# Six row buffers from the start of the expert gathers, weights in smaller pieces, and a new pacing table

## The chip, the cores and the metric

The kernel runs on one core of a Trainium2 chip. Its engines are TensorE (PE, with the weight loads as PEld), VectorE (DVE), ScalarE (ACT) and GpSimd (POOL); SyncE's queue (SP) issues most transfers. The metric is the device time of one execution in microseconds, and the kernel before is given by the median of three runs.

## The reference

One decoder block on 1024 tokens of width 1024, float32:

```
h = rms_norm(x);  proj = h @ w_in                    # 9232 columns
o_sb  = stick_breaking_attention(q, k, v)            # 8 heads of 128
o_gdn = gated_delta_rule(silu(conv(...)))            # 8 heads of 128, gates b and a
x = x + (sigmoid(g1) * (o_sb @ w1) + sigmoid(g2) * (o_gdn @ w2)) @ w_out
h = rms_norm(x)
# PEER: per token and head the best 16 of 128 x 128 experts (product keys)
expert, gate = route(h @ w_q, keys1, keys2)          # 8 heads x 16 = 128 experts a token
act = gelu(sum(h * u_tab[expert]))                   # 16384 rows of 1024 in each table
x = x + sum(gate * act * v_tab[expert])
```

## The kernel before, in words

The tokens are done in two halves of 512. A half goes through the stick-breaking heads (`sb_pair`), the delta-rule heads (`gdn_head`), the gate logits, the merge of both branches with their weights, the output projection, the norm ahead of the experts, and the routing (`route`, `route_block`). Matmuls take float32 operands split into a high and a low part, three products each (`mm3`); ACT makes the high part and DVE the low part (`split`, lines 63 and 64).

A weight slab of 1024 x 256 is loaded by `load_w` in two transfers of 512 KB into `w_raw` (two buffers of 4 KB a partition), split into `w_hi` and `w_lo` (two buffers each). There are 56 slabs in each half.

The expert part is done in two ways. Four of the eight token blocks (2, 3, 6, 7) are *dense*: `gate_table` writes a table of gates for all 16384 experts, and `dense` runs through all 128 groups of 128 experts: 24 matmuls for the scores of one group, 24 for its values. One group needs on DVE the low parts of the U and V slabs, the product with the gates (L915), the low part of the result (L906) and on average one addition to `d_acc` (L974). The other four blocks (0, 1, 4, 5) are *gathered* by `gather_rows`: for each of 128 expert columns POOL fetches 128 rows of the U table (512 KB, an indirect DMA, L1016) and DVE multiplies and sums them (L1019); then the same with the V table (L1021). That makes 4 x 256 = 1024 row fetches. Rows of block 0 exist when the first half is routed, so all rows run beside the second half and the dense part. Each row fetch lands in one of the buffers of `self.row_bufs` in turn: four of 4 KB a partition, and two more (`gp2`) while the dense loop runs.

What sets the order: the program is put into one order per engine by a scheduler that goes by priorities and its own costs. The rows get the lowest priority (`self.later(1000000)`), and a pacing table says how many of them become due at each step of the other work. `gather(phase)` adds `PACE[phase]` to `self.due`, and for each whole row puts one into the program, to stand on DVE behind the last DVE instruction issued so far (`self.behind`). The second half and the dense part call it 64 times in the stick-breaking heads, 80 in the delta rule, 16 each in logits, merge, output projection and routing, 64 in the gate tables and 128 in the dense loop. Rows left over at the end follow last. Each engine executes its order as written: an instruction that waits holds up all behind it on that engine, and so does a transfer in SP's queue that waits for its buffer.

In the second half's stick-breaking heads the keys and values of the first half come back from memory into `ko` and `vo` (256 KB each, two buffers). `gdn_head` keeps its tiles in the pool `gc`, two buffers a name, but one for `g_at` and `g_vn`. The residual `x2` has three of its four blocks in the pool `xp`, loaded during the merge, and the fourth in `fn`, loaded in front of the output projection. The raw V slabs of the dense part lie in the pool `up`, the split ones in `vp`, which opens after the routing buffers are given back (`gctx.close()`).

Of the kernel before, what the change touches and what calls it, by code (L numbers as in the profile page):

```python
# [7 lines left out]
F32 = mybir.dt.float32  # L8
# [10 lines left out]
P = 128  # L19
D = 1024  # L20
S = 1024
H = 8
TH = 512
NTB = TH // P
GT = 32
GQ = 4
KD = D // P
CB = 256
EPS = 1e-6

PACE = dict(sb=2.2, gdn=1.5, logits=2.5, merge=2.5, out=0.5, route=0, table=0.1, dense=5.25)
NEG = -1e30
C_Q, C_K, C_V = 0, 1024, 2048
C_GQ, C_GK, C_GV, C_GZ = 3072, 4096, 5120, 6144
# [4 lines left out]
class Block:  # L39
# [48 lines left out]
    def load_w(self, src, c0):  # L88


        hi = self.wp.tile([P, KD, CB], F32R, name="w_hi")
        lo = self.wp.tile([P, KD, CB], F32R, name="w_lo")
        for k0 in range(0, KD, 4):
            raw = self.wraw.tile([P, 4, CB], F32, name="w_raw")
            self.nc.sync.dma_start(raw, src[c0 // CB][:, k0:k0 + 4])
            for k in range(k0, k0 + 4, 2):
                self.split(hi[:, k:k + 2], lo[:, k:k + 2], raw[:, k - k0:k - k0 + 2])
        return hi, lo

    def load_ba(self):  # L100

        hi, lo = [self.wp.tile([P, KD, CB], F32R, name=f"w_{a}")[:, :, 0:16] for a in ("hi", "lo")]
        raw = self.wraw.tile([P, 4, CB], F32, name="w_raw").rearrange("p a b -> p (a b)")[:, 0:16 * KD]
        raw = raw.rearrange("p (k n) -> p k n", k=KD)
        self.nc.sync.dma_start(raw, self.i["w_ba"])
        self.split(hi, lo, raw)
        return hi, lo
# [233 lines left out]
    def sb_pair(self, half, pair, kqv):  # L341
        nc = self.nc
        k, q, v = kqv
        for h in range(2):
            kts = [k[:, h, j * P:(j + 1) * P] for j in range(NTB)]
            vs = [v[:, j, h * P:(h + 1) * P] for j in range(NTB)]
            if half:
                ko = self.ch.tile([P, TH], F32, name="ko", bufs=2)
                nc.sync.dma_start(ko, self.k_old[pair][:, h])
                vo = self.ch.tile([P, NTB, P], F32, name="vo", bufs=2)  # L350
                nc.sync.dma_start(vo, self.v_old[pair][:, :, h * P:(h + 1) * P])
                kts = [ko[:, j * P:(j + 1) * P] for j in range(NTB)] + kts
                vs = [vo[:, j] for j in range(NTB)] + vs
            self.sb_attend(half, pair * 2 + h, q[:, h], kts, vs)
# [96 lines left out]
    def gdn_head(self, half, head, G, r):  # L451
        nc, pool, mm = self.nc, self.ch, self.nc.tensor.matmul
        qT, kT, vT, sz = r["q"], r["k"], r["v"], r["z"]
        f = lambda a: a.rearrange("p a b -> p (a b)")
        tb_sl = lambda a, c: a[:, c * P:(c + 1) * P]
        col = lambda nm, c: G[nm][:, c, head:head + 1]
        W = lambda nm, **kw: pool.tile([P, NTB, P], F32, name=nm, **kw)
# [43 lines left out]
        M = W("g_M")  # L501
# [4 lines left out]
        TT, TN = W("g_TT"), W("g_TN")  # L506
# [30 lines left out]
        pq = pg()  # L537
        for c in range(NTB):
            mm(pq[:, c], tb_sl(kT, c), tb_sl(qT, c), start=True, stop=True)
        at = W("g_at", bufs=1)  # L540
        nc.vector.tensor_tensor(at, pq, dec, op=OP.mult)

        vn = W("g_vn", bufs=1)
        p2 = pg()
        for c in range(NTB):
            nc.tensor.transpose(p2[:, c], tb_sl(vT, c), self.ident)
# [307 lines left out]
    def dense(self, hx, blks, G, routes, gctx):  # L854
# [3 lines left out]
        W = nb * P  # L858
# [4 lines left out]
        with ExitStack() as ctx:  # L863
            pool = lambda *a, **k: ctx.enter_context(self.tc.tile_pool(*a, reuse_waits="tile", **k))
            up = pool(name="up", bufs=2)
# [63 lines left out]
            def values(vp):  # L929

                k = len(Vs)
                e1, dh = k // (2 * G) * G + k % G, k // G % 2
                raw = up.tile([P, 2, 512], F32, name="v_raw")
                nc.sync.dma_start(raw, V[e1 // 2, dh])
                v2 = [vp.tile([P, 2, 512], F32R, name=f"d_v{a}", bufs=VB // 2) for a in range(2)]
                self.split(v2[0], v2[1], raw)
                Vs.extend([[a[:, q] for a in v2] for q in range(2)])
# [19 lines left out]
            gctx.close()  # L957
            vp = pool(name="vp", bufs=2)
            acc = vp.tile([P, nb, D], F32, name="d_acc", bufs=1)
            gp2 = pool(name="gp2", bufs=1)  # L960
            self.row_bufs += [(gp2, f"gb_row{4 + k}") for k in range(2)]
            for k in range(0, VB, 2):
                values(vp)
            for k in range(LEAD):
                weigh(vp)
            for k in range(2 * NE1):
# [11 lines left out]
                if k % 2 == 1:  # L978
# [6 lines left out]
                    self.gather("dense")  # L985
                    if len(Vs) < 2 * NE1:
                        values(vp)
            del self.row_bufs[4:]
            for n, blk in enumerate(blks):
                nc.sync.dma_start(self.out[0, blk * P:(blk + 1) * P, :], acc[:, n])  # L990

# [1 line left out]
    def gather_rows(self, blks):  # L993

        nc = self.nc
        n = H * 16
        self.row_bufs = [(self.gp, f"gb_row{k}") for k in range(4)]
        turn = 0
        for blk in blks:
            h2 = self.gp.tile([P, D], F32, name="gb_h2", bufs=1)  # L1000
            nc.sync.dma_start(h2, self.h2_d[blk])
            act = self.gp.tile([P, n], F32, name="gb_act")
            ix = self.expert[blk]
            acc = None
            for p in range(2 * n):
                if p == n:
                    self.acts(nc.scalar.activation(act, act, AF.Gelu))
                    self.back_to_exp()
                    nc.vector.tensor_tensor(act, act, self.gate[blk], op=OP.mult)
                    acc = self.gp.tile([P, D], F32, name="gb_h2", bufs=1)  # L1010
                    nc.sync.dma_start(acc, self.x2_d[blk])
                pool, name = self.row_bufs[turn % len(self.row_bufs)]
                turn += 1
                r = pool.tile([P, D], F32, name=name, bufs=1)
                q = p % n
                nc.gpsimd.indirect_dma_start(out=r, out_offset=None, in_=self.i["peer_u" if p < n else "peer_v"][0],  # L1016
                                             in_offset=bass.IndirectOffsetOnAxis(ap=ix[:, q:q + 1], axis=0))
                if p < n:
                    i = nc.vector.scalar_tensor_tensor(r, r, 1.0, h2, op0=OP.mult, op1=OP.mult, accum_out=act[:, q:q + 1])  # L1019
                else:  # L1020
                    i = nc.vector.scalar_tensor_tensor(acc, r, act[:, q:q + 1], acc, op0=OP.mult, op1=OP.add)  # L1021
                if self.anchor is not None:
                    self.behind(i, self.anchor)
                if p == 2 * n - 1:
                    nc.sync.dma_start(self.out[0, blk * P:(blk + 1) * P, :], acc)
                yield
# [34 lines left out]
    def half(self, half, hx, new_h, st, x2_in):  # L1061

        nc, tc = self.nc, self.tc
        tp = lambda name, **k: tc.tile_pool(name=name, bufs=1, reuse_waits="tile", **k)
        if x2_in is None:
            self.mixers(half, hx)
        xctx = ExitStack()
        xp = xctx.enter_context(tp("xp", side="right"))
        x2 = [xp.tile([P, D], F32, name=f"x2{tb}") for tb in range(3)]
        if x2_in is None:  # L1070
            with tp("mo") as mo:
                mg = new_h()
                self.merge(half, mg, x2, mo)
        hb = st.enter_context(tp("hb"))
        with tp("rt") as rt:
            with tp("fn") as fn:
                x2 += [fn.tile([P, D], F32, name=f"x2{tb}") for tb in range(3, NTB)]
                if x2_in is None:
                    self.load_x(half, x2, range(3, NTB))
                    self.out_proj(half, mg, x2)  # L1080
                else:
                    for tb in range(NTB):
                        nc.sync.dma_start(x2[tb], x2_in[0, half * TH + tb * P:half * TH + (tb + 1) * P])
                self.keysT = rt.tile([P, H, 2, P], F32, name="keysT")
                nc.sync.dma_start(self.keysT, self.i["keys_t"])
                hf = [hb.tile([P, KD, TH], F32R, name=f"hf{a}") for a in range(2)]
                self.ffn_norm(half, x2, hf, fn)
            xctx.close()
            with tp("rq") as rq:
                routes = self.route(half, hf, rq)  # L1090
                if half == 0 and x2_in is None:
                    with tp("nin") as nin:
                        hx = new_h()
                        self.norm_in(1, hx, nin)
        return hf, hx, routes


def block_kernel(tc, ins, out, x2_in=None, dense_blks=(2, 3, 6, 7), G=8):
    b = Block(tc, ins, out)
    b.dense_blks = list(dense_blks)  # L1100
    nc = tc.nc
    with ExitStack() as ctx:
        pool = lambda *a, **k: ctx.enter_context(tc.tile_pool(*a, **k))
# [19 lines left out]
        with ExitStack() as rctx:  # L1123
            right = lambda name, bufs: rctx.enter_context(tc.tile_pool(name=name, bufs=bufs, side="right"))
            cm = right("cm", 1)
            hp = right("hp", 1)
            b.wp = right("wp", 2)
            b.wraw = right("wraw", 2)
            new_h = lambda: [hp.tile([P, KD, TH], F32R, name=f"h{a}") for a in range(2)]
            with tc.tile_pool(name="ctmp", bufs=1) as tp:  # L1130
                b.consts_first(cp, tp)
# [47 lines left out]
```

## Time and profile before

| | us |
|---|---|
| median of 3 runs (3879.04 to 3883.69) | 3883.02 |
| profiled execution | 3877.26 |
| its span, first to last instruction | 3875.4 |
| PE busy | 3596.4 |
| DVE busy | 3077.5 |
| ACT busy | 1740.7 |
| POOL busy | 1356.6 |

The second half starts its heads near 1015 us, the gate tables run from 2142 to 2373 us and the dense loop from there to the end. In the rows, an engine's busy time is followed by the number of its instructions in brackets; PEclk is the granted TensorE clock as a share of full speed; a group of instructions shows its busy time, the mean of one in ns, and the idle time of its engine just before it with what ended that.

### The profile page before, as it was taken

How to read it: one execution, taken by the hardware profiler on the slowest of the kernel's cores; microseconds unless marked ns; L12 is line 12 of the kernel's file. 1: busy time of each engine (PE TensorE's matmuls, PEld its weight loads, DVE VectorE, ACT ScalarE, POOL GpSimd, SP SyncE). 2: the span in 40 equal slices, each digit the busy share in tenths (PEclk: the TensorE clock that was granted, in tenths of full speed). 3: DMA queues.
4: the chain of work that ended last, by engine and by line, in shares of the span. 5: the costliest groups of instructions: out<-in, count | busy, mean ns of one | idle time of the engine just before them, and what ended most of it. 6: DMA issues, size and time to landing. Idle time of an engine off the chain costs nothing.

```text
span 3875.4 us, 53560 instructions
## 1 busy us (share of the span) xinstructions
PE 3596.4 (93%) x18936; PEld 2983.8 (77%) x18936; DVE 3077.5 (79%) x6196; ACT 1740.7 (45%) x3846; POOL 1356.6 (35%) x1034
## 2 busy tenths in 40 slices
PE   8999999999999999998878877999999999999996
PEld 7878888788777688886667666787778787788785
DVE  5345554349988878888879998899898899899898
ACT  6755554333777655553322786222222322222221
POOL 0000000000044332223442003666666665676665
PEclk9999999999999999999989999999999999999998
DMA  4221113553377756558985568999999999999998
GB/s 121 88 82 50 55 50 115 174 186 93 96 256 265 246 191 192 191 182 290 325 307 170 158 185 289 353 361 358 334 365 358 345 371 365 348 364 374 353 359 312
DMA packets 344205, 937.49 MB, mean 242 GB/s; under 512 B 41984, under 2 KB 121088, under 8 KB 339712
## 3 DMA queue, kind: packets, MB, share of 16 engines
q0 software_dynamic: 147456, 536.94, 38.8%
q1 hardware_dynamic: 196480, 397.13, 30.1%
q8 instruction: 149, 2.44, 0.3%
q14 instruction: 120, 0.98, 0.1%
HBM read 864.22 MB, written 69.21 MB: 241 GB/s over the span
## 4 chain that ended last, share of the span: by engine, by line
PE 42%; issue 20%; POOL 12%; DVE 11%; DMA 10%; ACT 4%; SPq 0%; POOLq 0%; DVEq 0%; ACTq 0%
POOL gb_row L1016 12%; PE mm L72 6%; PE mm L74 6%; PE mm L73 6%; DMA gb_row<-peer_v,expert 5%; PE pc L848 3%; DMA gb_row<-peer_u,expert 3%; PE mm L885 2%; PE pz L532 2%; PE pz L526 2%; DVE gb_row L1019 2%; DVE w_lo L64 2%; PE mm L887 1%; PE pc L317 1%; PE pz L295 1%
## 5 line engine op out<-in xcount | busy, mean ns | idle before, releaser
L1016 POOL DMA_INDIRECT gb_row<-peer_u,expert x512 | 693.6, 1355 | 1848.2 <-DVE expert L793 1012.8
L1016 POOL DMA_INDIRECT gb_row<-peer_v,expert x512 | 661.9, 1293 | 656.4 <-DVE gb_h L1021 408.8
L1019 DVE SCALAR_TENSOR_TENSOR gb_row<-gb_row,gb_h 128x1024 f32<-128x1024 f32 x512 | 614.0, 1219 | 133.2 <-DMA gb_row<-peer_u,expert 109.7
L1021 DVE SCALAR_TENSOR_TENSOR gb_h<-gb_row,gb_act,gb_h 128x1024 f32<-128x1024 f32 x512 | 657.7, 1285 | 73.7 <-DMA gb_row<-peer_v,expert 50.4
L885 PE MATMUL mm<-hf,ut 128*128 128x512 f32 x2048 | 491.2, 391 | 6.9 <-DMA hf<-hd 6.9
L919 ACT CAST d_a<-u_act 128x512 fp32r<-128x512 f32 x128 | 79.2, 621 | 926.5 <-DVE u_act L915 917.7
L885 PEld LDWEIGHTS mm<-hf,ut 128*128 128x128 f32 x2048 | 386.1, 189 | 87.7 <-issue 7.6
L64 DVE TENSOR_TENSOR w_lo<-w_raw,w_hi 128x512 fp32r<-128x512 f32 (+1 forms) x450 | 297.6, 682 | 163.9 <-ACT w_hi L63 125.9
L63 ACT CAST w_hi<-w_raw 128x512 fp32r<-128x512 f32 (+1 forms) x450 | 262.1, 620 | 286.2 <-PE mm L73 122.6
L72 PE MATMUL mm<-h,w_hi 128*128 128x512 f32 (+1 forms) x784 | 322.9, 412 | 3.0 <-ACT pj L598 3.0
L74 PE MATMUL mm<-h,w_lo 128*128 128x512 f32 (+1 forms) x784 | 320.6, 409 | 0.0
L73 PE MATMUL mm<-h,w_hi 128*128 128x512 f32 (+1 forms) x784 | 319.7, 408 | 0.0
L72 PE MATMUL pz<-d_v,d_a 128*128 128x512 f32 x680 | 272.8, 401 | 41.2 <-DVE d_acc L974 30.1
L72 PE MATMUL mm<-w_hi,h 128*128 128x256 f32 x1024 | 299.8, 293 | 8.5 <-DVE x L647 5.7
L74 PE MATMUL mm<-w_hi,h 128*128 128x256 f32 x1024 | 294.0, 288 | 4.0 <-DVE h L64 4.0
L73 PE MATMUL mm<-w_lo,h 128*128 128x256 f32 x1024 | 295.1, 288 | 1.0 <-DVE w_lo L64 0.9
L74 PE MATMUL pz<-d_v,d_a 128*128 128x512 f32 x680 | 270.4, 398 | 0.0
L73 PE MATMUL pz<-d_v,d_a 128*128 128x512 f32 x680 | 270.4, 398 | 0.0
L887 PE MATMUL mm<-hf,ut 128*128 128x512 f32 x1024 | 257.0, 391 | 2.5 <-DVE ut L64 2.5
L887 PEld LDWEIGHTS mm<-hf,ut 128*128 128x128 f32 x1024 | 192.8, 188 | 42.8 <-DVE ut L64 3.3
L72 PEld LDWEIGHTS mm<-w_hi,h 128*128 128x128 f32 x1024 | 199.5, 195 | 16.3 <-DVE x L647 6.4
L73 PEld LDWEIGHTS mm<-w_lo,h 128*128 128x128 f32 x1024 | 199.7, 195 | 6.7 <-issue 3.8
(327 smaller groups left out, 7947.9 us busy)
## 6 DMA issues: line engine op xcount, KB each, us to landing
w_raw<-w_in SPq DMA_DIRECT2D x144, 512.0 KB
u_raw<-u_t SPq DMA_DIRECT2D x128, 512.0 KB
v_raw<-v_t SPq DMA_DIRECT2D x128, 512.0 KB
g_d<-gt_stg SPq DMA_DIRECT2D x16, 2048.0 KB
d_g<-g_d SPq DMA_DIRECT2D x31, 1024.0 KB
w_raw<-peer_w_q SPq DMA_DIRECT2D x32, 512.0 KB
gl<-pj SPq DMA_DIRECT2D x32, 256.0 KB
th<-gl SPq DMA_DIRECT2D x32, 256.0 KB
```

The costliest lines, as they stand in the source:

```text
L63: nc.scalar.copy(hi, src)
L64: nc.vector.tensor_tensor(lo, src, hi.bitcast(F32), op=OP.subtract)
L72: mm(out, l[0], r[0], start=first, stop=False)
L73: mm(out, l[0], r[1], start=False, stop=False)
L74: mm(out, l[1], r[0], start=False, stop=last)
L848: self.last_gate = mm(pg[:, u - u0], o2[:, u], o1[:, u], start=True, stop=True)
L885: mm(ps, ut[0][:, k], hx[a][:, k, x0:], start=k + a == 0, stop=False)
L887: mm(ps, ut[1][:, k], hx[0][:, k, x0:], start=False, stop=k == KD - 1)
L919: nc.scalar.copy(hi, act)
L1016: nc.gpsimd.indirect_dma_start(out=r, out_offset=None, in_=self.i["peer_u" if p < n else "peer_v"][0], in_offset=bass.IndirectOffsetOnAxis ...
L1019: i = nc.vector.scalar_tensor_tensor(r, r, 1.0, h2, op0=OP.mult, op1=OP.mult, accum_out=act[:, q:q + 1])
L1021: i = nc.vector.scalar_tensor_tensor(acc, r, act[:, q:q + 1], acc, op0=OP.mult, op1=OP.add)
```

## The change

- `row_bufs` has six buffers from the start; `gp2` is gone. All six stay in use to the end.
- `w_raw` has three buffers of 2 KB a partition for two of 4 KB; a slab comes in four transfers of 256 KB.
- `ko` and `vo` have one buffer each. In `gdn_head`, `at` is written into `M` and `vn` into `TN`, whose last readers stand ahead of it.
- `xp` holds two blocks of `x2` for three; blocks 2 and 3 lie in `fn`.
- The raw V slabs lie in `vp`.
- The pacing table is new; with its numbers of calls, 404.8 rows are due ahead of the dense loop for 355.2.

```diff
-PACE = dict(sb=2.2, gdn=1.5, logits=2.5, merge=2.5, out=0.5, route=0, table=0.1, dense=5.25)
+PACE = dict(sb=2.4, gdn=2.0, logits=2, merge=2, out=0.5, route=0, table=0.3, dense=4.85)
...
-        for k0 in range(0, KD, 4):
-            raw = self.wraw.tile([P, 4, CB], F32, name="w_raw")
-            self.nc.sync.dma_start(raw, src[c0 // CB][:, k0:k0 + 4])
-            for k in range(k0, k0 + 4, 2):
-                self.split(hi[:, k:k + 2], lo[:, k:k + 2], raw[:, k - k0:k - k0 + 2])
+        for k in range(0, KD, 2):
+            raw = self.wraw.tile([P, 2, CB], F32, name="w_raw")
+            self.nc.sync.dma_start(raw, src[c0 // CB][:, k:k + 2])
+            self.split(hi[:, k:k + 2], lo[:, k:k + 2], raw)
...
-                ko = self.ch.tile([P, TH], F32, name="ko", bufs=2)
+                ko = self.ch.tile([P, TH], F32, name="ko", bufs=1)
-                vo = self.ch.tile([P, NTB, P], F32, name="vo", bufs=2)
+                vo = self.ch.tile([P, NTB, P], F32, name="vo", bufs=1)
...
-        at = W("g_at", bufs=1)
+        at = M
-        vn = W("g_vn", bufs=1)
+        vn = TN
...
-                raw = up.tile([P, 2, 512], F32, name="v_raw")
+                raw = vp.tile([P, 2, 512], F32, name="v_raw")
...
-            gp2 = pool(name="gp2", bufs=1)
-            self.row_bufs += [(gp2, f"gb_row{4 + k}") for k in range(2)]
-            del self.row_bufs[4:]
-        self.row_bufs = [(self.gp, f"gb_row{k}") for k in range(4)]
+        self.row_bufs = [(self.gp, f"gb_row{k}") for k in range(6)]
...
-        x2 = [xp.tile([P, D], F32, name=f"x2{tb}") for tb in range(3)]
+        x2 = [xp.tile([P, D], F32, name=f"x2{tb}") for tb in range(2)]
-                    self.load_x(half, x2, range(3, NTB))
+                    self.load_x(half, x2, range(2, NTB))
...
-            b.wraw = right("wraw", 2)
+            b.wraw = right("wraw", 3)
```

The first place is DVE in front of the second half's merge. `o` are the low parts of the attention output that the merge multiplies, `gb_row` the fetched rows, `part` the first product of the merge. Before, the last `o` stands 25 rows ahead of this piece:

```order
L1021 SCALAR_TENSOR_TENSOR gb_h_13437<-gb_row_16645,gb_act,gb_h_13437 128x1024
L783 TENSOR_TENSOR r_scr<-r_tab,r_i 128x1024
L1021 SCALAR_TENSOR_TENSOR gb_h_13437<-gb_row_16648,gb_act,gb_h_13437 128x1024
L785 TENSOR_REDUCE r_fa<-r_scr 128x64
L624 TENSOR_TENSOR part<-mm,th 128x512
```

The same place on DVE of the kernel after the change:

```order
L1017 SCALAR_TENSOR_TENSOR gb_h_13596<-gb_row_16613,gb_act,gb_h_13596 128x1024
L64 TENSOR_TENSOR o_18521<-o_raw,o_18520 128x512
L1017 SCALAR_TENSOR_TENSOR gb_h_13596<-gb_row_16632,gb_act,gb_h_13596 128x1024
L64 TENSOR_TENSOR o_18521<-o_raw,o_18520 128x512 x2
L1017 SCALAR_TENSOR_TENSOR gb_h_13596<-gb_row_16635,gb_act,gb_h_13596 128x1024
L64 TENSOR_TENSOR o_18521<-o_raw,o_18520 128x512
L1017 SCALAR_TENSOR_TENSOR gb_h_13596<-gb_row_16654,gb_act,gb_h_13596 128x1024
L1017 SCALAR_TENSOR_TENSOR gb_h_13596<-gb_row_16657,gb_act,gb_h_13596 128x1024
L64 TENSOR_TENSOR o_18521<-o_raw,o_18520 128x512
L1017 SCALAR_TENSOR_TENSOR gb_h_13596<-gb_row_16779,gb_act,gb_h_13596 128x1024
L623 TENSOR_TENSOR part<-mm,th 128x512 x2
```

Between the last delta-rule head's output (L585) and the first `part`, 5 rows stood before and 17 stand now, and the `o` parts stand among them.

The second place is DVE late in the dense loop, from one product with the gates (`u_act`) to the next, before:

```order
L915 TENSOR_TENSOR u_act<-u_act,d_g 128x512
L1019 SCALAR_TENSOR_TENSOR gb_row_30013,gb_act<-gb_row_30013,gb_h_29578 128x1024
L906 TENSOR_TENSOR d_a_29998<-u_act,d_a_29997 128x512
L1019 SCALAR_TENSOR_TENSOR gb_row_30016,gb_act<-gb_row_30016,gb_h_29578 128x1024
L1019 SCALAR_TENSOR_TENSOR gb_row_30091,gb_act<-gb_row_30091,gb_h_29578 128x1024
L1019 SCALAR_TENSOR_TENSOR gb_row_30094,gb_act<-gb_row_30094,gb_h_29578 128x1024
L64 TENSOR_TENSOR d_v_30109<-v_raw,d_v_30108 128x1024
L1019 SCALAR_TENSOR_TENSOR gb_row_30097,gb_act<-gb_row_30097,gb_h_29578 128x1024
L1019 SCALAR_TENSOR_TENSOR gb_row_30100,gb_act<-gb_row_30100,gb_h_29578 128x1024
L1019 SCALAR_TENSOR_TENSOR gb_row_30103,gb_act<-gb_row_30103,gb_h_29578 128x1024
L915 TENSOR_TENSOR u_act<-u_act,d_g 128x512
```

And the same group after:

```order
L914 TENSOR_TENSOR u_act<-u_act,d_g 128x512
L1015 SCALAR_TENSOR_TENSOR gb_row_30477,gb_act<-gb_row_30477,gb_h_29781 128x1024
L905 TENSOR_TENSOR d_a_30462<-u_act,d_a_30461 128x512
L1015 SCALAR_TENSOR_TENSOR gb_row_30552,gb_act<-gb_row_30552,gb_h_29781 128x1024
L1015 SCALAR_TENSOR_TENSOR gb_row_30555,gb_act<-gb_row_30555,gb_h_29781 128x1024
L1015 SCALAR_TENSOR_TENSOR gb_row_30558,gb_act<-gb_row_30558,gb_h_29781 128x1024
L64 TENSOR_TENSOR d_v_30570<-v_raw,d_v_30569 128x1024
L1015 SCALAR_TENSOR_TENSOR gb_row_30561,gb_act<-gb_row_30561,gb_h_29781 128x1024
L1015 SCALAR_TENSOR_TENSOR gb_row_30564,gb_act<-gb_row_30564,gb_h_29781 128x1024
L64 TENSOR_TENSOR ut_30600<-u_raw,ut_30599 128x1024
L914 TENSOR_TENSOR u_act<-u_act,d_g 128x512
```

Seven rows stood in this group before, six now. The number of rows that DVE has behind it at marks of its order:

| mark on DVE | before | after |
|---|---|---|
| end of the stick-breaking heads, second half | 100 | 108 |
| last delta-rule head's output | 228 | 237 |
| first product of the merge | 233 | 254 |
| last product of the merge | 268 | 285 |
| first gate table | 323 | 343 |
| 8th product with the gates in the dense loop | 362 | 384 |
| 64th | 657 | 686 |
| 128th | 995 | 996 |

The third place is SP's queue at the start of the dense loop, where `g_d` is the gate table's way to memory and `d_g` its way back. Before (the first two V slabs were issued ahead of the gate tables):

```order
L851 DMA g_d<-gt_stg 128x32x128 x3
L870 DMA u_raw<-u_t 128x1024
L900 DMA d_g<-g_d 128x512 x4
L934 DMA v_raw<-v_t 128x1024
L900 DMA d_g<-g_d 128x2048 x2
```

And after:

```order
L850 DMA g_d<-gt_stg 128x32x128 x3
L869 DMA u_raw<-u_t 128x1024
L933 DMA v_raw<-v_t 128x1024 x2
L899 DMA d_g<-g_d 128x512 x4
L933 DMA v_raw<-v_t 128x1024
```

Two V slabs of 512 KB moved from ahead of the gate tables to between U and the gates.

## Rows read from the trace of the kernel before

**Rows 1.** The page, part 1: busy time, share and count of each engine.

```profile
span 3875.4 us, 53560 instructions
...
PE 3596.4 (93%) x18936; PEld 2983.8 (77%) x18936; DVE 3077.5 (79%) x6196; ACT 1740.7 (45%) x3846; POOL 1356.6 (35%) x1034
```

**Rows 2.** Stages of the second half: stretch, then busy times, clock, DMA.

```profile
core 0: us, PE busy (x) PEld busy (x) DVE busy (x) ACT busy (x) POOL busy (x), PEclk, DMA share, GB/s
1015.00:1385.00 370.00, 342.25 (x1760) 260.61 (x1759) 320.87 (x684) 272.60 (x699) 151.39 (x130) 0.96 0.72 238
1385.00:1775.00 390.00, 373.52 (x2431) 322.08 (x2431) 321.63 (x722) 206.69 (x543) 109.70 (x100) 0.99 0.60 192
1775.00:1873.00 98.00, 84.83 (x337) 66.49 (x335) 80.57 (x158) 36.84 (x62) 33.92 (x27) 0.92 0.89 306
...
1926.00:2008.00 82.00, 53.06 (x391) 50.53 (x389) 61.70 (x123) 19.06 (x40) 33.00 (x29) 0.83 0.89 313
2008.00:2142.00 134.00, 116.63 (x540) 93.28 (x540) 128.39 (x599) 34.74 (x62) 36.72 (x27) 0.93 0.58 189
...
2373.00:2441.00 68.00, 55.47 (x252) 44.76 (x252) 47.12 (x69) 26.82 (x42) 31.33 (x23) 0.95 1.00 361
2441.00:3095.00 654.00, 623.93 (x2686) 511.60 (x2685) 584.79 (x727) 178.96 (x230) 418.66 (x297) 0.97 0.94 353
3095.00:3818.00 723.00, 705.62 (x3080) 580.29 (x3079) 671.93 (x786) 200.15 (x257) 466.77 (x338) 0.99 0.96 360
```

**Rows 3.** DVE's row instructions, 2441 to 3095 us: busy, mean ns | idle before.

```profile
L1021 DVE SCALAR_TENSOR_TENSOR gb_h<-gb_row,gb_act,gb_h 128x1024 f32<-128x1024 f32 x145 | 186.5, 1286 | 24.7 <-DMA gb_h<-x2d 13.2 <-DMA gb_row<-peer_v,expert 9.2
L1019 DVE SCALAR_TENSOR_TENSOR gb_row<-gb_row,gb_h 128x1024 f32<-128x1024 f32 x150 | 178.5, 1220 | 34.9 <-DMA gb_row<-peer_u,expert 22.8 <-DMA gb_h<-h2d 11.5
```

**Rows 4.** The same, 3095 to 3818 us.

```profile
L1021 DVE SCALAR_TENSOR_TENSOR gb_h<-gb_row,gb_act,gb_h 128x1024 f32<-128x1024 f32 x210 | 270.3, 1287 | 18.3 <-DMA gb_row<-peer_v,expert 11.9 <-DMA gb_h<-x2d 2.7
L1019 DVE SCALAR_TENSOR_TENSOR gb_row<-gb_row,gb_h 128x1024 f32<-128x1024 f32 x128 | 152.1, 1220 | 19.3 <-DMA gb_row<-peer_u,expert 9.1 <-DMA gb_h<-h2d 8.5 <-issue 1.2
```

**Rows 5.** A stretch of the dense loop, columns as in Rows 2.

```profile
3400.00:3500.00 100.00, 100.00 (x443) 82.80 (x442) 94.96 (x145) 29.65 (x37) 72.18 (x51) 1.00 0.99 377
```

**Rows 6.** Products with the gates (L915) in both stretches.

```profile
2441.00:3095.00 654.00, 38.10 (x56) 0.97 0.94 353
3095.00:3818.00 723.00, 43.76 (x64) 0.99 0.96 360
```

**Rows 7.** DVE's row instructions, 1015 to 1385 us.

```profile
L1019 DVE SCALAR_TENSOR_TENSOR gb_row<-gb_row,gb_h 128x1024 f32<-128x1024 f32 x127 | 154.2, 1219 | 38.0 <-DMA gb_row<-peer_u,expert 36.9
```

**Rows 8.** DVE's row instructions, 1385 to 1775 us, the larger group.

```profile
L1021 DVE SCALAR_TENSOR_TENSOR gb_h<-gb_row,gb_act,gb_h 128x1024 f32<-128x1024 f32 x100 | 127.8, 1278 | 18.0 <-DMA gb_row<-peer_v,expert 17.8
```

**Rows 9.** DVE's row instructions, 1926 to 2008 us.

```profile
L1019 DVE SCALAR_TENSOR_TENSOR gb_row<-gb_row,gb_h 128x1024 f32<-128x1024 f32 x29 | 35.2, 1222 | 17.0 <-DMA gb_row<-peer_u,expert 17.0
```

**Rows 10.** PE in order of time at the merge: start, length, [idle before <-releaser].

```profile
1810.83 0.50 PE L72 MATMUL mm<-o,w_hi 128*128 128x512 f32 x1
...
1842.61 0.53 PE L72 MATMUL mm<-o,w_hi 128*128 128x512 f32 x1 [3.55 <-DVE part L624]
...
1873.52 0.79 PE L72 MATMUL mm<-o,w_hi 128*128 128x512 f32 x1 [6.72 <-ACT o L63]
```

**Rows 11.** The chain that ended last, pieces: start, length, what.

```profile
21.52 4.17 DMA w_raw<-w_in
...
754.18 3.47 DMA o_raw<-ogd
...
1778.88 9.72 DMA o_raw<-osb
```

**Rows 12.** PE at the first value matmul of the dense loop.

```profile
2415.74 0.80 PE L72 MATMUL pz<-d_v,d_a 128*128 128x512 f32 x1 [7.63 <-ACT d_a L919]
```

**Rows 13.** The page, part 5: groups of the weight split.

```profile
L64 DVE TENSOR_TENSOR w_lo<-w_raw,w_hi 128x512 fp32r<-128x512 f32 (+1 forms) x450 | 297.6, 682 | 163.9 <-ACT w_hi L63 125.9
L63 ACT CAST w_hi<-w_raw 128x512 fp32r<-128x512 f32 (+1 forms) x450 | 262.1, 620 | 286.2 <-PE mm L73 122.6
```

More of the change, by code (lines that the diff above doesn't have):

```diff
@@ L102, in load_ba @@
         hi, lo = [self.wp.tile([P, KD, CB], F32R, name=f"w_{a}")[:, :, 0:16] for a in ("hi", "lo")]
-        raw = self.wraw.tile([P, 4, CB], F32, name="w_raw").rearrange("p a b -> p (a b)")[:, 0:16 * KD]
+        raw = self.wraw.tile([P, 2, CB], F32, name="w_raw").rearrange("p a b -> p (a b)")[:, 0:16 * KD]
         raw = raw.rearrange("p (k n) -> p k n", k=KD)
@@ L1076, in half @@
             with tp("fn") as fn:
-                x2 += [fn.tile([P, D], F32, name=f"x2{tb}") for tb in range(3, NTB)]
+                x2 += [fn.tile([P, D], F32, name=f"x2{tb}") for tb in range(2, NTB)]
                 if x2_in is None:
-                    self.load_x(half, x2, range(3, NTB))
+                    self.load_x(half, x2, range(2, NTB))
                     self.out_proj(half, mg, x2)
```

## The prediction

> **What bounds the kernel now.** I read the page first: PE is busy 93% of the span and DVE 79% [rows 1]. These are averages, so I then cut the second half and the dense part into stages [rows 2] and asked in each which engine has no slack. The first half carries no rows and is left aside.
>
> In the dense loop I cut at the 8th, 64th and 128th product with the gates, so that the two stretches hold 56 and 64 expert groups [rows 6]. In the first, DVE is busy 584.79 us and idle in front of a row instruction for 24.7 + 34.9 us [rows 2, 3]: 644 of 654 us. In the second it is 671.93 + 18.3 + 19.3 = 709.5 of 723 us [rows 2, 4]. So DVE works or waits for a fetched row nearly all the time. PE is not far behind: where nothing holds it, it issues 443 matmuls in 100 us, 0.2257 us each [rows 5]. Its 2686 and 3080 matmuls [rows 2] would take 606 and 695 us, so PE loses 48 and 28 us. These two losses cap whatever fewer rows can give there.
>
> In the stick-breaking heads DVE is busy 320.87 us and idle 38.0 us in front of rows, 359 of 370 us [rows 2, 7]: DVE's queue again. In the norm ahead of the experts it is 61.70 + 17.0 = 78.7 of 82 us [rows 2, 9]. The routing has DVE busy 128.39 of 134 us. The delta-rule heads are PE's: 373.52 of 390 us at a clock of 0.99 [rows 2].
>
> **The change part by part.** The pacing table makes 50 rows due earlier, but DVE's written order moves only about 20: at the first gate table 343 rows are behind it for 323, at the 8th product 384 for 362. What is due and finds no room slides on. From the 8th to the 64th product the order has 302 rows for 295, and from there to the 128th 310 for 338; after that the same tail.
>
> Dense, second stretch: 28 rows fewer at (270.3 + 152.1)/338 = 1.25 us [rows 4] are 35 us of DVE. PE's floor lets 28 through. The waits at a change of block (8.5 + 2.7 us [rows 4]) stay, so I take 8 us of stalls as left: **-20**, bounds -28 (the floor) and -5 (the row fetches themselves set the pace).
>
> Dense, first stretch: 7 rows more at (186.5 + 178.5)/295 = 1.24 us [rows 3], with DVE full: **+9**, bounds 0 and +16, which is 7 rows at the stretch's own pace of 654/295 = 2.2 us. The upper end asks that a row's whole loop from fetch to release is the pace, the lower that 5 us of waits go.
>
> Start of the dense loop (2373 to 2441 us): two rows more, and two V slabs now issued just ahead of the first gates in SP's queue; against that six row buffers where there were four until the loop, in a stretch where DVE is busy 47.12 of 68 us [rows 2]. PE waits here 7.63 us for the first weighted activations [rows 12]. I take **0**, bounds -8 (that wait goes) and +8 (two slabs at the 4.17 us of a 512 KB load [rows 11] stand in front of the gates).
>
> Stick-breaking heads: 8 rows more at 1.22 us are +10. Two buffers more start each fetch two rows earlier. How much of the 38.0 us of waiting goes I read from the dense loop, which has six buffers already: 11.9 + 9.1 us on fetches over 338 rows, 22.8 + 9.2 over 295, that is 0.06 to 0.11 us a row [rows 3, 4], against 0.30 here. At 0.1 us, 135 rows wait 14 us: -24. Together **-14**, bounds -24 and +10 (the waits stay, the rows are added). `ko` and `vo` with one buffer are needed only in the last four of eight steps of a head, so their 256 KB load has half a head to land: 0.
>
> Delta rule: PE is the bound, one row more, 18.0 us of row waits [rows 8] that mostly hide behind PE: **-3**, bounds -10 and +4. `vn` in `TN` and `at` in `M` could hold up the next head, but in the written order its steps still alternate with this head's chunks: 0.
>
> Merge: between the last head's output and the first product of the merge DVE now has 17 rows for 5, 12 x 1.28 = 15.4 us more [mean of rows 8], and the low parts of `o` stand among them. PE reached its first `o` at 1810.83 and lost 3.55 and 6.72 us to such parts later [rows 10]; DVE is busy 80.57 of 98 us [rows 2]. Beyond the first product DVE's order is shorter by 4 rows, so some comes back: **+8**, bounds 0 and +22 (15.4 and one more wait like the 6.72).
>
> Norm ahead of the experts: 17.0 us of waits over 29 rows; at 0.1 us a row 14 go. `x2` block 2 now loads as late as block 3, one more 512 KB in front of the output projection: +4 by its 4.17 us [rows 11]; and it stands in SP's queue ahead of weights. **-8**, bounds -14 and +6. Routing: 3 rows more (+4) against the waits of the same kind: 0.
>
> Weights in pieces: 56 slabs in a half take four transfers for two, the casts and low parts are the same instructions of 512 columns. With `w_hi` and `w_lo` double, a slab is split while PE works on the one before; that hides a late piece except where DVE is the bound. **0**, bounds -3 and +10 outside the rival below.
>
> The sum is -20 + 9 + 0 - 14 - 3 + 8 - 8 + 0 = **-28 us**. The profiled execution took 3877.26 us (span 3875.4 [rows 1] and 1.9 around it), 5.8 us less than the median, so I forecast 3883 - 28 = **3855 us**.
>
> **The rivals.** *The fourth piece of a slab makes DVE wait* (the other side). With three buffers the fourth piece can be fetched only when the first has been split. A 256 KB transfer took 3.47 us [rows 11], its cast 0.62; DVE reaches the fourth low part two low parts (2 x 0.68 us [rows 13]) after the first: 4.1 - 1.4 = 2.7 us of waiting a slab, more where a load takes the 9.72 us of the merge's start [rows 11]. Where DVE is the bound, the second half has 9 slabs in the stick-breaking heads, 8 in the merge, 4 in the output projection and 8 in the routing: 29 x 2.7 = 78 us at most. From 28/2.7, some 10 slabs on, nothing is gained; at 17 of 29 the time is 3883 + 18 = **3901 us**. Against it: in the written order of the routing DVE does a slab's fourth low part one head later, beside the first three of the next slab, so its fetch has a head's time.
>
> The Trainium skill's page "DMA: Bandwidth & Descriptors" speaks against small pieces too: its section Bandwidth advises transfers of 1 MiB and more, and its section on the anatomy of one DMA gives each a fixed 2.0 us beside its bytes. By that the 224 further transfers would carry an estimated 448 us of fixed time if none of it overlapped. This trace agrees that half the bytes take far more than half the time (3.47 us for 256 KB, 4.17 for 512 KB [rows 11]); whether it overlaps decides the rival above.
>
> *No gain.* If the waits in front of rows come from loaded transfers (a DMA share of 0.72 in the heads, 0.89 in merge and norm [rows 2]) and not from the number of buffers, only a quarter of the waits goes: the heads give +10 - 9 = +1, the norm +4 - 4 = 0, the delta rule 0, the merge +8, the dense loop +9 - 20: -2 us, **3881 us**. For it: the fetches wait just where much else moves. Against it: the dense loop runs at shares of 0.94 and 0.96 with the smallest waits a row.
>
> *A larger gain.* All bounds at their good end but the floor: -28 in the second stretch, 0 in the first, -8, -24, -10, -14 and 0 for the merge: -84, **3799 us**. It needs DVE's relief to reach the end in every stage, while PE is within 4 to 8% of its own floor in most.
>
> That the change does not do what its words say is already in the sum: 20 rows move, not 50.
>
> **How the numbers follow.** My forecast (10 to 50 us faster, 3833 to 3873) gets 0.58, the larger gain 0.12, no gain 0.16, the late pieces 0.14. Differences within 0.2% (7.8 us) can't be told from none: faster 0.70, same 0.16, slower 0.14. The range for 8 in 10 cuts half of the larger gain and the upper part of the slow case: 3815 to 3896 us.
>
> **What would show it.** In the second half's heads the idle time in front of rows falls from 38 to near 14 us, and the heads end near 1371 us for 1385. The first product of the merge comes some 10 us later after the last head's output, with PE idle on `o`. From the 8th to the 64th product 654 us becomes some 663, from there to the 128th 723 becomes some 703 with PE's matmuls back to back and DVE idle with nothing to wait for. I am wrong if DVE waits on ACT's `w_hi` in merge and routing, if row waits a row in the heads stay at 0.3 us, or if the second dense stretch stays above 715 us.

## The result and the profile after

The changed kernel took 3910.0 us (median of 6 runs, 3901.75 to 3922.67) against 3877.8 us for the kernel before on the same chip (6 runs): ratio 1.0086, 95% interval 1.0062 to 1.0110. It is slower; the forecast was 3855 us. The profiled execution, 3901.75 us, is the fastest of the six, so its profile shows 24.5 of the 32 us between the medians. The line numbers in the second part of the kernel are one to four lower than before.

The page of the changed kernel, part 1, beside [rows 1]:

```profile
span 3900.0 us, 54096 instructions
...
PE 3601.0 (92%) x18936; PEld 2986.5 (77%) x18936; DVE 3080.6 (79%) x6196; ACT 1748.1 (45%) x3845; POOL 1375.4 (35%) x1034
```

The two busiest engines hardly work longer: PE and DVE gain 4.6 and 3.1 us. Most of the 24.6 us of span is waiting. The table cuts both traces at the same instructions: the last copy of a routing query in the first half, DVE's first product of the stick-breaking heads, its first product of the delta rule's levels, the last head's output (L585, then L584), the last product with `th` in the merge (L626, then L625), the last sum of the output projection (L655, then L654), and the products with the gates.

| stretch | before, us | after, us | difference |
|---|---|---|---|
| to the first half's last routing query | 966.7 | 977.7 | +11.0 |
| to the second half's first stick-breaking product | 57.5 | 64.7 | +7.2 |
| stick-breaking heads, to the first delta level | 371.5 | 382.7 | +11.2 |
| delta rule | 379.8 | 375.9 | -3.9 |
| last delta output to last merged part | 150.7 | 174.8 | +24.1 |
| output projection and norm | 66.0 | 61.3 | -4.7 |
| routing, tables, start of the dense loop | 448.6 | 452.8 | +4.2 |
| 8th to 64th product with the gates | 654.6 | 658.9 | +4.3 |
| 64th to 128th | 722.7 | 696.2 | -26.5 |
| tail | 57.3 | 54.9 | -2.4 |

The stage windows after, answering to [rows 2] (stretch, busy times of PE, PEld, DVE, ACT, POOL, clock, DMA share, GB/s): heads, delta rule, norm ahead of the experts, and the two dense stretches.

```profile
1033.00:1412.00 379.00, 344.65 (x1738) 257.91 (x1738) 323.26 (x688) 272.74 (x696) 164.50 (x135) 0.95 0.73 241
1412.00:1801.00 389.00, 375.62 (x2445) 323.75 (x2445) 329.16 (x726) 207.24 (x546) 120.94 (x108) 0.99 0.62 198
...
1976.00:2058.00 82.00, 54.90 (x389) 53.12 (x390) 63.74 (x124) 19.68 (x40) 38.55 (x30) 0.80 0.95 342
...
2490.00:3149.00 659.00, 628.33 (x2703) 515.12 (x2703) 596.02 (x712) 178.29 (x227) 420.25 (x302) 0.98 0.95 356
3149.00:3845.00 696.00, 695.43 (x3067) 575.28 (x3066) 638.54 (x757) 203.32 (x257) 442.29 (x310) 1.00 0.95 353
```

In the last dense stretch PE is busy 695.43 of 696 us and DVE has slack (638.54 us busy): that term came as said. In the heads DVE is busy 2.4 us more in a window that is 9 us longer. What DVE waits for there: the low parts of the weights before, then the two largest groups of its instructions after (count, busy us, mean ns, idle before, releaser), against [rows 7]:

```profile
L64 DVE TENSOR_TENSOR w_lo<-w_raw,w_hi 128x512 fp32r<-128x512 f32 x54 | 36.2, 681 | 0.0
...
L1015 DVE SCALAR_TENSOR_TENSOR gb_row<-gb_row,gb_h 128x1024 f32<-128x1024 f32 x128 | 153.9, 1220 | 7.3 <-DMA gb_row<-peer_u,expert 6.8
L64 DVE TENSOR_TENSOR w_lo<-w_raw,w_hi 128x512 fp32r<-128x512 f32 x54 | 36.8, 685 | 19.5 <-ACT w_hi L63 19.5
```

The wait in front of rows fell from 38.0 to 7.3 us, further than forecast. But the low parts of the weights now wait 19.5 us for their casts, before 0.0, and the casts wait 48.3 us for the loads, before 18.6. The chain that ended last in these heads, its shares by line before and after, and pieces of it after (start, length, what):

```profile
by line: DMA gb_row<-peer_u,expert 14.4%; issue 13.8%; DVE gb_row L1019 8.8%; PE pc L317 8.3%; PE pz L295 8.1%; POOL gb_row L1016 5.3%; DVE w_lo L64 4.4%; PE pz L306 3.3%; PE pc L319 2.8%; PE mm L74 2.8%; PE pz L307 2.6%; PE mm L73 2.6%; PE
...
by line: DMA w_raw<-w_in 15.5%; issue 9.1%; DVE gb_row L1015 8.7%; PE pz L294 7.6%; PE pc L316 7.0%; DMA gb_row<-peer_u,expert 3.5%; DMA osb<-sb_a 3.1%; PE pz L305 3.0%; DVE w_lo L64 2.9%; ACT sb_hi L63 2.7%; ACT w_hi L63 2.5%; ACT sb_a L31
...
1090.09 0.65 DVE w_lo L64
1090.76 3.71 DMA w_raw<-w_in
1094.49 0.62 ACT w_hi L63
...
1193.88 0.60 DVE w_lo L64
1194.51 6.79 DMA w_raw<-w_in
1201.33 0.63 ACT w_hi L63
1201.98 0.69 DVE w_lo L64
```

This is the loop of the late piece: a low part frees a buffer, a load of 4 to 7 us follows, then cast and low part of the slab's last piece. Before, the first place in this chain was the fetch of rows with 14.4%, and no weight load was among its 195 longest pieces. Over the whole kernel: the casts of the weights after, answering to [rows 13], and what the casts waited for weight loads in all (us, times), before and then after:

```profile
L63 ACT CAST w_hi<-w_raw 128x512 fp32r<-128x512 f32 (+1 forms) x450 | 270.0, 621 | 447.9 <-DMA w_raw<-w_in 135.2 <-PE mm L73 119.4 <-DMA w_raw<-peer_w_q 84.7
...
  ACT w_hi L63: 103.4, 39
...
  ACT w_hi L63: 282.5, 103
```

There are 112 slabs. One wait is hardly longer than before (2.74 us for 2.65), but there are 103 for 39. Counted in order along ACT, 69 of the 103 (193 us) stand ahead of the fourth piece of a slab, 29 in the first half and 40 in the second; before there was none at that place, since the third and fourth piece came with one load. The other loss is the merge. SP's loads of `o`, first and last issue, before and then after:

```profile
L612 SPq DMA_DIRECT2D o_raw<-osb x8: 319/320/926, 1777.9 to 1793.7; - x8
L599 SPq DMA_DIRECT2D gl<-pj x13: 319/327/626, 1721.4 to 1842.9; - x13
```

```profile
L598 SPq DMA_DIRECT2D gl<-pj x16: 319/327/424, 1703.7 to 1839.9; - x16
L611 SPq DMA_DIRECT2D o_raw<-osb x8: 319/320/526, 1844.0 to 1862.7; - x8
```

Before, they start 65 us ahead of the last stored logits (`gl`), and merge products fill PE among the logits; after, they start behind them, and PE waits for the split `o`. PE's waits on it, before (1773 to 1890 us) and after (1801 to 1920 us), in all, times, longest (against [rows 10]):

```profile
PE mm L72 <- ACT o L63: 9.1, 3, 6.7
...
PE mm L72 <- ACT o L63: 26.0, 3, 13.1
```

The reason lies in the addresses of the built program, which no trace shows. The merge's tiles (62 KB a partition) start 8 KB higher behind the six row buffers, and their last 448 bytes, in the fourth `th`, now lie over the pool `pj`, the scratch that logits and projections share. Before, 5,696 bytes lay between.

### The profile page after: what moved, and what is told of

Read it like the earlier page. It is cut to its first block, busy times and chain, and to the rows that moved or that the text cites. A ratio compares the mean times of both kernels' runs of the same rounds, so it can differ in the third digit from the quotient of the medians.

```text
span 3900.0 us, 54096 instructions
## 1 busy us (share of the span) xinstructions
PE 3601.0 (92%) x18936; PEld 2986.5 (77%) x18936; DVE 3080.6 (79%) x6196; ACT 1748.1 (45%) x3845; POOL 1375.4 (35%) x1034
## 4 chain that ended last, share of the span: by engine, by line
PE 38%; issue 22%; DVE 12%; POOL 12%; DMA 10%; ACT 6%; POOLq 0%; DVEq 0%; SPq 0%; ACTq 0%
POOL gb_row L1012 12%; PE mm L72 6%; PE mm L73 6%; PE mm L74 6%; DMA gb_row<-peer_v,expert 3%; DMA w_raw<-w_in 2%; PE pz L531 2%; PE pc L847 2%; PE pz L525 2%; DVE gb_row L1015 2%; DVE w_lo L64 1%; DVE gb_h L1017 1%; PE mm L884 1%; PE pz L521 1%; PE pz L294 1%
## 5 line engine op out<-in xcount | busy, mean ns | idle before, releaser
L1012 POOL DMA_INDIRECT gb_row<-peer_u,expert x512 | 702.9, 1373 | 1850.2 <-DVE expert L792 1030.3
L1012 POOL DMA_INDIRECT gb_row<-peer_v,expert x512 | 671.4, 1311 | 661.1 <-DVE gb_h L1017 431.6
L63 ACT CAST w_hi<-w_raw 128x512 fp32r<-128x512 f32 (+1 forms) x450 | 270.0, 621 | 447.9 <-DMA w_raw<-w_in 135.2
L72 PEld LDWEIGHTS mm<-w_hi,h 128*128 128x128 f32 x1024 | 201.8, 197 | 18.7 <-issue 6.2
L74 PEld LDWEIGHTS mm<-w_hi,h 128*128 128x128 f32 x1024 | 201.5, 197 | 7.8 <-DVE h L64 4.8
```

The source lines that it names most:

```text
L63: nc.scalar.copy(hi, src)
L72: mm(out, l[0], r[0], start=first, stop=False)
L74: mm(out, l[1], r[0], start=False, stop=last)
```

## The experiments

Each run was timed beside the kernel before; the ratios are to it.

**Is it the 448 bytes?** In the changed kernel:

```diff
-                    th = pool.tile([P, TH], F32, name="th", bufs=4)
+                    th = pool.tile([P, TH], F32, name="th", bufs=3)
```

> The changed kernel with three gate buffers (th) in the merge instead of four, so that the merge's tiles end below the logits' buffers (they overlapped by 448 bytes) and stand among the logits again in the order. Theory (overlap): the 11 us of the first half's merge and the 24 us of the second's come from the merge being put behind all logits; this gives most of it back, some 25 to 35 us, ratio to the kernel before 1.000 to 1.003, and the second half from the last delta head to the last merged part falls from 174.8 to about 150 us. Rival (weight pieces): the merge is late because the weights come in three 2 KB pieces; then it stays within 5 us of 174.8 and the ratio at 1.007 to 1.010.

3906.1 us, ratio 1.0076 (1.0059 to 1.0092). The merge came back as the theory said: the last merged part stands 24 us earlier than in the changed kernel, the last delta output to that part took 158.5 us for 174.8, and PE's wait on `o` there (1793 to 1895 us) is

```profile
PE mm L72 <- ACT o L63: 5.9, 1, 5.9
```

SP's first load of `o` again starts 67 us ahead of the last stored logits; the runs with five row buffers below, which keep four `th` and have no overlap, start it 65 to 72 us ahead. But the time hardly moved, because the wait had been used: DVE had done 48 rows between the last delta output and the last merged part, now 36. Ten of the 12 rows came back in the dense stretches, 667 + 701 us for 659 + 696; norm, routing and the start of the dense loop took some 8 us more. So the overlap costs about 0.1% net, and by the two intervals no more than 0.4%: the theory had the place right and the price wrong. By the ratio alone the rival (1.007 to 1.010) would stand, and it has a share: the merge keeps 8 of its 24 us.

**Is it the weight pieces?** The kernel before with three 2 KB pieces, shown here, and with four (`right("wraw", 4)`); `load_ba` likewise:

```diff
-        for k0 in range(0, KD, 4):
-            raw = self.wraw.tile([P, 4, CB], F32, name="w_raw")
-            self.nc.sync.dma_start(raw, src[c0 // CB][:, k0:k0 + 4])
...
+        for k in range(0, KD, 2):
+            raw = self.wraw.tile([P, 2, CB], F32, name="w_raw")
+            self.nc.sync.dma_start(raw, src[c0 // CB][:, k:k + 2])
...
-            b.wraw = right("wraw", 2)
+            b.wraw = right("wraw", 3)
```

> The kernel before with nothing changed but the weights: three pieces of 2 KB a partition in place of two of 4 KB, so 6 KB instead of 8 wait ready. Theory (reserve): a tile of weights has four such pieces, the fourth can be asked for only when the first is split; ACT's wait for weight pieces in the stick-breaking stretch of the second half rises from 18.6 us to 40 or more, the norm and heads of the second half get 7 to 25 us longer, and the whole is slower by 15 to 40 us, ratio 1.004 to 1.010. Rival (crowding): the changed kernel's weights are late because of its bursts of rows; then this one stays within 0.2%, with the wait under 25 us.

> The kernel before with four weight pieces of 2 KB: the pieces as small as in the change, the reserve as large as before (8 KB). Theory (reserve): within 0.2% of the kernel before, or faster by up to 10 us, since a piece's buffer is free after one split instead of two; ACT's wait for weight pieces in the stick-breaking stretch stays under 25 us. Rival (size: twice as many transfers on SP's queue, each with its own start): as slow as with three pieces, ratio 1.004 to 1.010.

Three pieces: 3932.0 us, 1.0137 (1.0117 to 1.0156), even more than expected. Four: 3879.9 us, 0.9998 (0.9985 to 1.0010). The number of transfers is the same in both; only the 6 or 8 KB that lie ready differ. The casts, three pieces and then four:

```profile
L63 ACT CAST w_hi<-w_raw 128x512 fp32r<-128x512 f32 (+1 forms) x450 | 271.1, 621 | 439.1 <-PE mm L73 116.4 <-DMA w_raw<-w_in 112.3 <-DMA w_raw<-peer_w_q 85.7
```

```profile
L63 ACT CAST w_hi<-w_raw 128x512 fp32r<-128x512 f32 (+1 forms) x450 | 263.3, 620 | 291.9 <-PE mm L73 152.8 <-PE mm L74 42.9 <-DMA w_raw<-peer_w_q 42.5
```

A slab is 8 KB a partition. With all of it ahead the casts wait for weight loads no more than before (83 us in 36 waits); with three quarters they wait 275 us in 113, and 68 of these waits stand ahead of a slab's fourth piece, 30 in the first half and 38 in the second, where four pieces have 14.

**The table alone, and the table undone.** The new `PACE` line in the kernel before; the old one in the changed kernel.

> The kernel before with nothing changed but the table of rows per step. Theory: the second dense stretch falls from 722.7 to about 698 us as in the changed kernel (six buffers were there already), and the rows that move to the heads and the delta rule wait there on four buffers for 0 to 15 us more; ratio 0.993 to 0.998. Rival (buffers): without six buffers the moved rows cost in the heads and the delta rule what they save behind; ratio 0.999 to 1.003, with the stick-breaking stretch of the second half over 300 us against 295.1.

> The changed kernel with the old table of rows per step: six buffers alone. Theory (the second dense stretch's 26 us come from 39 instead of 42 rows to eight experts, which the table sets): that stretch goes back to about 720 us, the first to about 645, and the time rises by 5 to 20 us, ratio to the kernel before 1.010 to 1.014. Rival (the buffers move the rows, whatever the table says, since with four buffers the new table left the rows of heads, delta rule and tables at 128, 100 and 73): rows and stretches stay within 5 rows and 6 us of the changed kernel, ratio 1.007 to 1.010.

The table alone: 3907.6 us, 1.0086 (1.0068 to 1.0104), slower than either side said. Heads, delta rule, merge and tables hold the same rows as before (128, 100, 40, 73): with four buffers nothing moved ahead. The loss is in the first dense stretch, which took 688 us for 654.6 and waited for its rows:

```profile
DVE gb_row L1019 <- DMA gb_row<-peer_u,expert: 38.5, 28, 3.5
DVE gb_h L1021 <- DMA gb_row<-peer_v,expert: 24.6, 19, 5.1
```

against 22.8 and 9.2 us before [rows 3]. Eleven rows more explain 14 of the 33 us; why the fetches ran later is open. The second stretch, with ten rows fewer, gained nothing (725.6 us). The old table with six buffers: 3928.9 us, 1.0124 (1.0101 to 1.0146), as the theory said: heads, delta rule and merge keep 136, 101 and 48 rows, which the buffers set, but the start of the dense loop has 8 rows for 23, and the last stretch takes 732 us with 338 rows. With six buffers the table is worth 0.4%.

**The small cuts alone**, in the kernel before: `ko` and `vo` with `bufs=1`, `at = M`, `vn = TN`.

> The kernel before with the old keys and values in one buffer each and the delta rule's at and vn written over M and TN. Theory: neither is on the path; the second half's heads stay at 295 +/- 4 us, the delta rule at 380 +/- 4, ratio 0.999 to 1.001. Rival: one buffer for the old keys holds SP's queue and the weights behind it, and the cuts carry part of the heads' 8 us; ratio 1.002 to 1.005, heads over 300.

3882.1 us, 1.0005 (0.9994 to 1.0017): nothing, heads 295.1 and delta rule 383.5 us.

**Five row buffers pay for themselves.** In the changed kernel, with the two 4 KB pieces back:

```diff
+            gp2 = pool(name="gp2", bufs=1)
+            self.row_bufs += [(gp2, "gb_row5")]
...
+            del self.row_bufs[5:]
...
-        self.row_bufs = [(self.gp, f"gb_row{k}") for k in range(6)]
+        self.row_bufs = [(self.gp, f"gb_row{k}") for k in range(5)]
...
-            b.wraw = right("wraw", 3)
+            b.wraw = right("wraw", 2)
```

> The changed kernel with five row buffers from the first routing on (a sixth opened for the dense expert pass, as before) and the weights back in two pieces of 4 KB; its shorter merge overlap is gone too, so the merge stands among the logits. Theory (reserve): up to the second half's norm the marks come as in the kernel before (1992 us, not 2037), with 133 or so rows in the second half's heads; the dense expert pass takes 1355 to 1385 us, and the whole 3845 to 3880 against 3878, ratio 0.992 to 1.001. Rival (the moved rows themselves cost what they save, as in the kernel before with the new table alone): first dense stretch over 680 us, ratio 1.004 to 1.009.

> As the run with five row buffers and two 4 KB weight pieces, with the old table of rows per step. If the table alone decides the dense stretches, the second one is about 720 us and the time 3870 to 3885; if the buffers decide, within 5 us of the run with the new table. As the new table alone slowed the kernel before by 0.9%, this may be the faster of the two: ratio 0.995 to 1.002.

With the new table 3856.8 us, 0.9949 (0.9929 to 0.9968); with the old one 3853.3 us (3846.3 to 3854.0), 0.9928 (0.9910 to 0.9947). **Both beat both kernels**; between them the table makes no difference in the whole that can be told, though it decides the dense stretches (667 + 712 us with 307 + 323 rows, and 655 + 729 with 294 + 338). Heads and delta rule with the new table:

```profile
1016.00:1380.00 364.00, 338.84 (x1756) 258.18 (x1755) 323.65 (x691) 273.06 (x701) 157.26 (x133) 0.97 0.73 247
1380.00:1754.00 374.00, 370.56 (x2434) 319.80 (x2433) 317.90 (x715) 205.49 (x543) 111.09 (x98) 1.00 0.60 194
```

PE is busy 370.56 of 374 us in the delta rule. From the first stick-breaking product to the last delta output it is 728 us, before 751. The rows are as many (227, before 228) and wait less: 23.9 us in the heads and 6.3 in the delta rule for 38.0 and 18.0.

**What is a sixth buffer worth, and more reserve?** Five buffers with the three 2 KB pieces; and the kernel before with the small cuts, `x2` as in the change, and three 4 KB pieces.

> The changed kernel with five row buffers to the dense pass instead of six (a sixth opened there), its three 2 KB weight pieces kept; it differs from the run with five buffers and two 4 KB pieces in the pieces alone, and has no overlap of merge and logits buffers. Theory (the cost of the pieces adds to that of the buffers): 48 to 58 us slower than that run, 3905 to 3915 us, ratio 1.007 to 1.010, so the sixth buffer is worth about nothing. Rival (the sixth buffer carries much of the gain): 3920 us or more, ratio over 1.011.

> The kernel before with three 4 KB weight pieces (12 KB ready in place of 8); the room comes from the single buffers of old keys and values and the delta rule's reuse, which moved nothing by themselves (ratio 1.0005), and from two x2 tiles in the early pool instead of three. Theory A (a reserve of one whole tile of weights is what counts): a half tile more gives at most 8 us, ratio 0.997 to 1.001. Theory B (each KB of reserve is worth as much as the 2 KB that were taken away, 53 us): faster by 20 us or more, ratio under 0.995.

Five buffers, three pieces: 3894.0 us, 1.0031 (1.0015 to 1.0047), faster than both sides said. It differs from the run with 4 KB pieces by 0.82%, some 32 us, and from the run without the overlap, which has the sixth buffer and one `th` fewer, by 0.45%: the sixth buffer costs. In the profiles of those two that is eight rows more in the heads, where the time to the first delta level is 384.5 us for 369.4, and the gate tables end 20 us later; the dense stretches give back 22 (1368 for 1390). These profiles come out even (the one with five buffers is the slowest of its six executions); where the 0.45% lies they do not show. Three 4 KB pieces: 3876.5 us, 0.9990 (0.9978 to 1.0002), and no weight load is left among the three largest waits ahead of the casts (all together 22.7 us):

```profile
L63 ACT CAST w_hi<-w_raw 128x512 fp32r<-128x512 f32 (+1 forms) x450 | 261.2, 620 | 241.6 <-PE mm L73 156.2 <-PE mm L74 30.6 <-issue 27.0
```

So the waits on weight loads before (103 us) cost nothing that can be told (at most 0.2%), and the further 180 after cost 32 to 53 us: half a slab beyond the whole one is worth next to nothing, a quarter less is dear. Six row buffers with a whole slab of weights were not run, nor the move of the raw V slabs into `vp` by itself; the start of the dense loop took 67.9 us for 68.0.

## Why the prediction was wrong

**The step that failed is "Weights in pieces", taken as 0 with bounds -3 and +10.** By itself it measured +53 us on four row buffers and some +32 on five. The mechanism stood among the rivals, with its loop and 3901 us, at a chance of 0.14; the range of 8 in 10 ended at 3896, below that rival's own time. It was set aside on two readings. That the doubled `w_hi` and `w_lo` hide a late piece holds only while the split runs a slab ahead; the chain in the heads shows ACT and DVE held there. And 3.47 us for a load was an early, light place: on the chain in the heads it took 3.7 to 7.1.

The rival had the loop right, and its place: ahead of a slab's fourth low part DVE waits at 47 slabs, 2.2 us each (before: at one), for the 2.7 us forecast. Its sum was chosen, not derived: it took 17 of 29 slabs of the second half. The time lost to the pieces, 53 us over 112 slabs, is 0.5 us a slab, so most of the waiting was covered. That the mean of ACT's 103 waits, 2.74 us, is near 2.7 shows nothing, as it was 2.65 before.

**The first half was left aside** because it carries no rows. It carries as many slabs: 18.2 us of the 24.6 were lost before the second half's heads began, 11 of them at the merge (9 come back without the overlap) and 7 at the start of the next half, where ACT waits 16.3 us for `w_in` pieces (before 3.1). By itself the run with three pieces is 15 us behind there.

The row terms were right in sign and mostly in size. Dense, second stretch: -20 forecast, -26.5 measured, to PE's floor; the profiles with 338 rows there spread from 722.7 to 731.6 us, and the one before is the lowest. First stretch: +9, measured +4.3. Start: 0, and 67.9 us for 68.0. Delta rule: -3, measured -3.9, with row waits of 2.1 us for 18.0 [rows 8]. Heads: the waits fell by more than the forecast 24 us, but the late weights took it and more, +8 for -14 up to the last head; with the full reserve heads and delta rule give 23 us against the forecast 17. Norm ahead of the experts: the row waits fell from 17.0 to 2.8 us [rows 9] and 9.5 us of waiting for `w_hi` came, of the kind named as a sign of being wrong; output projection and norm gave -4.7 for -8. Routing: 0 forecast, +4 to the last query.

**Merge:** +8 forecast, +24.1 measured, beyond the bound of 22, with PE idle on `o` as named. Its first product came 28 us later after the last head's output, for some 10 forecast. Most of the cause was another one: not 12 rows in front of the low parts, but the whole merge put behind the logits by memory that it shares. Without the overlap 16 of the 24 us come back. The other 8 go with the pieces: the runs with three pieces and no overlap take 158.5 to 164.6 us there, those with 4 KB pieces 149.9 to 153.0; but four 2 KB pieces took 161.1 in their profile, so whether reserve or size does it is open. The written order had shown the later start; it was read as DVE's queue alone. As the wait was filled with 12 rows, the whole paid little for the overlap.

The 20 rows instead of 50 were right, but it takes both parts to move them: ahead of the 8th product with the gates stand 362 rows before, 362 with the new table alone, 363 with six buffers and the old table, 384 with both, and 374 with both when the overlap is gone.

The Trainium skill's page "DMA: Bandwidth & Descriptors" gives, in the section on the anatomy of one DMA, a fixed 2.0 us for a transfer that GpSimd issues. The prediction put that on loads that SyncE issues. The run with four pieces has all 224 further transfers and is no slower (0.9998), so nothing of the estimated 448 us shows while a whole slab is ready. What decided was the reserve.

From run to run, each step one edit (with the sixth buffer also one `th`), the 0.86% are made up of: five buffers with cuts and table -0.5%, the weight reserve +0.8%, the sixth buffer +0.45%, the overlap +0.1%. These are differences of neighbouring runs, each uncertain by 0.2 to 0.3%, so that they add up proves nothing more. Why the sixth buffer costs stays open.

## What to carry to other kernels

When a change takes bytes from one ring of buffers to give them to another, compare the ring with one whole unit of what it feeds (here a slab of 8 KB): at the unit it was free to cut transfers in half and useless to add more; just below it the casts of 82 of 112 units waited for a load, for 29 before. Price that at every place the ring is used, the parts the change is not about too. And look at the addresses after a pool grows: 448 bytes of overlap turned the order of two stages around.

## What the hardware showed that was not expected

The length of a load depends on the place of use. In the run with five row buffers and three pieces the 256 KB weight loads took 3.0 us from issue to landing (median) in the first 680 us, at a DMA share of 0.27, and 5.5 us in the second half's heads, at 0.71. With five buffers and 512 KB loads it was 3.7 and 7.0 us: half the bytes took four fifths of the time at both places.

And the waits were not simply exchanged. In the heads, with three pieces and four row buffers, DVE waited 8.9 us for casts beside 29.0 for rows; with six, 19.5 beside 7.3; with five and whole 4 KB pieces, 0.4 beside 23.9. The small reserve made the wait, and the shorter row waits let more of it show.
